# Ordering a two-layer decoder trunk by the tile context's timeline model instead of its core model

## The chip, the cores and the metric

The kernel runs on one core of a Trainium2 chip. The metric is the device time of one execution in microseconds (us). The core has TensorE (PE, with a separate row PEld for its weight loads), VectorE (DVE), ScalarE (ACT), GpSimd (POOL) and SyncE (SP, which issues the DMA transfers here). Each engine works through its own list of instructions in order. An instruction that waits for a semaphore holds up everything behind it on its engine.

## The reference, cut to what matters

Two layers over x of 1024 tokens by 1024 features, all in float32:

```python
h = x @ w_in                                   # 1024 x 2912
o_sb   = stick_breaking_attention(q, k, v)     # 4 heads of 64, causal
o_mla  = mla_mixer(...)                        # 4 heads, causal softmax attention
o_rwkv = rwkv7_mixer(...)                      # 8 heads of 64, a linear recurrence over time
mix = concatenate([o_sb, o_mla, o_rwkv]) @ w_o
x = layer_norm(ALPHA * x + mix)
u_act, u_gate = split(x @ ffn_w_up, 2)
hid = gelu(causal_depthwise_conv(u_act)) * u_gate
x = layer_norm(ALPHA * x + hid @ ffn_w_down)
```

Stick-breaking attention multiplies each score's weight by the product of "keep" factors of all later keys, which is a scan along the keys. The recurrence is `state = state*w - (state@kk)*(kk*a) + v*k`, with the output `state @ r` at each of the 1024 steps.

## The kernel before

The code is one long Python function that emits instructions in program order inside a tile context. The tile context knows which instruction needs which tile, adds the semaphores, and then **chooses the order of instructions on each engine** with a model of the machine: among the instructions that its model holds ready, it takes the one that stands earliest in the program, shifted by the numbers of a table `PRIORITY` (L38 to L50; `rw_chain_q` 80 and `rw_chain_s` 40 go forward, `rw_chain_y2` -60 goes back). So the order on the chip comes from that model. [...]

Float32 products are made of three matmuls on split operands (`mm3`, L202 to L204: high by high, high by low, low by high), each 128x512. A name with `psmm` is such a matmul of a dense projection or of the feed-forward network (FFN).

A layer goes through these parts, named here as the prediction names them:

- **Prefix.** `phase_a` makes the projections of the softmax attention and of the recurrence, and for each of four feature tiles (`ft`) the first stage `rw_stage1` (transposes, then L662 on PE, masks on DVE at L665 and L666, then L674 on PE). The last L674 ends the prefix. The recurrence is done in chunks of 64 tokens, and each chunk needs the inverse of a triangular matrix. `rw_inv` makes it for a pair of feature tiles: on DVE a transposition L701, a forward substitution in small steps L705 and L706, and a transposition L726; then a row of hand-overs: PE L735, ACT L738, POOL L740, DVE L743, PE L752, ACT L755, PE L764 (on `LA<-xxd`, loaded by DMA L760), ACT L765, and DMA L768 to the DRAM buffer `psd`. It is run twice a layer, once within the prefix and once behind it.
- **Serial stretch.** `rw_chain(0)` runs the recurrence for the first pair of feature tiles: per step two DMA loads `PSl<-psd` L807 and `RBl<-rbd` L808, PE L820, DVE L821 and L822 with ACT L823, then the state `S`: PE L839, DVE L842, which the next step needs. The second inverse is interleaved with it.
- **Second chain.** `rw_chain(1)` needs the `psd` of the second inverse. In the program it stands among `proj_sb` (L260), the six dense projections of the stick-breaking attention: 288 `psmm` matmuls, which need nothing but x and weights.
- **Attention.** The softmax streams (`mla`, scores L202 to L204 and L539 into `pssc`) and the stick-breaking streams (`stick`: scores PE L376 and L377 into `pspq` and `pspy`, ACT L378, POOL L384, DVE L385, L387 and L388 on the tile `mexp`, then PE L327, which transposes `mexp`, ACT L328, PE L312).
- **Output projection and FFN.** `oproj` and `ffn`: thousands of `psmm` and `psps` matmuls.

The buffers bound how far work can be pulled forward: `pst` holds four projection results, `PSl` and `RBl` two steps, `mexp` three blocks, `wt4` six blocks.

## Time and profile before

| | |
|---|---|
| median of 3 runs (3151.39 to 3157.18) | 3154.57 us |
| the profiled execution's own time | 3154.05 us |
| its span in the trace | 3152.3 us |
| PE busy | 2993.2 us, 95% |
| DVE busy | 1796.4 us, 57% |
| ACT busy | 1058.6 us, 34% |
| POOL busy | 330.7 us, 10% |
| mean granted TensorE clock, share of full speed | 0.981 |

"Busy" is the time in which an engine had an instruction under way; the rest of the span it sat idle. The granted clock is the share of 2.4 GHz at which TensorE was allowed to run: 1.00 is 2.4 GHz all the time, 0.50 would be 1.2 GHz all the time. A mean over a stretch mixes the two levels. The span plus 1.75 us is the execution's time.

### The profile page before, as it was taken

How to read it: one execution, taken by the hardware profiler on the slowest of the kernel's cores; microseconds unless marked ns; L12 is line 12 of the kernel's file. 1: busy time of each engine (PE TensorE's matmuls, PEld its weight loads, DVE VectorE, ACT ScalarE, POOL GpSimd, SP SyncE). 2: the span in 40 equal slices, each digit the busy share in tenths (PEclk: the TensorE clock that was granted, in tenths of full speed). 3: DMA queues.
4: the chain of work that ended last, by engine and by line, in shares of the span. 5: the costliest groups of instructions: out<-in, count | busy, mean ns of one | idle time of the engine just before them, and what ended most of it. 6: DMA issues, size and time to landing. Idle time of an engine off the chain costs nothing. (4 is left out here: it accounts for less than half of the span.)

```text
span 3152.3 us, 42021 instructions
## 1 busy us (share of the span) xinstructions
PE 2993.2 (95%) x16572; PEld 2421.2 (77%) x16572; DVE 1796.4 (57%) x2842; ACT 1058.6 (34%) x1865; POOL 330.7 (10%) x346
## 2 busy tenths in 40 slices
PE   8998999988999999999999989999789999999998
PEld 6677777776888888888877767777678888888887
DVE  4587764876644444444746877567865444344436
ACT  5444343764122112222144443446532211122220
POOL 0112131132000000000001111311310000000000
PEclk9999899999999999999999999999899999999999
DMA  4344566323421111111234456662235111111111
GB/s 129 97 141 110 169 186 191 97 62 121 149 85 50 51 41 47 54 50 51 64 84 127 108 132 193 178 190 53 81 121 172 54 47 40 43 56 49 54 47 54
DMA packets 339284, 301.79 MB, mean 96 GB/s; under 512 B 25224, under 2 KB 304016, under 8 KB 339088
## 3 DMA queue, kind: packets, MB, share of 16 engines
q1 hardware_dynamic: 339088, 299.11, 32.1%
q8 instruction: 131, 2.15, 0.3%
q14 instruction: 65, 0.53, 0.1%
HBM read 208.87 MB, written 90.18 MB: 95 GB/s over the span
## 5 line engine op out<-in xcount | busy, mean ns | idle before, releaser
L202 PE MATMUL psmm<-xTh,whi 128*128 128x512 f32 x2144 | 852.9, 398 | 0.0
L204 PE MATMUL psmm<-xTh,wlo 128*128 128x512 f32 x2144 | 852.1, 397 | 0.0
L203 PE MATMUL psmm<-xTl,whi 128*128 128x512 f32 x2144 | 852.1, 397 | 0.0
L197 ACT CAST whi<-raw 128x1024 fp32r<-128x1024 f32 x152 | 159.9, 1052 | 1111.3 <-PE psmm L203 1076.1
L204 PEld LDWEIGHTS psmm<-xTh,wlo 128*128 128x128 f32 x2144 | 405.2, 189 | 93.2 <-issue 4.3
L202 PEld LDWEIGHTS psmm<-xTh,whi 128*128 128x128 f32 x2144 | 405.4, 189 | 92.9 <-issue 4.4
L203 PEld LDWEIGHTS psmm<-xTl,whi 128*128 128x128 f32 x2144 | 405.3, 189 | 92.8 <-issue 3.9
L198 DVE TENSOR_TENSOR wlo<-raw,whi 128x1024 fp32r<-128x1024 f32 x122 | 148.8, 1220 | 424.5 <-ACT whi L197 424.5
L1031 DVE TENSOR_TENSOR y<-y,psps 128x512 f32<-128x512 f32 x288 | 196.2, 686 | 171.8 <-PE psps L204 171.4
L202 PE MATMUL psps<-wdh,hh 128*128 128x512 f32 x672 | 266.8, 397 | 0.0
L203 PE MATMUL psps<-wdl,hh 128*128 128x512 f32 x672 | 263.1, 391 | 0.0
L204 PE MATMUL psps<-wdh,hl 128*128 128x512 f32 x672 | 260.1, 391 | 0.0
L894 POOL TENSOR_TENSOR lrs<-lrs,mhalf 128x1 f32<-128x1 f32 x32 | 29.1, 910 | 1637.7 <-DVE lrs L893 1637.7
L202 PEld LDWEIGHTS psps<-wdh,hh 128*128 128x128 f32 x672 | 126.1, 188 | 36.4 <-ACT hh L197 5.5
L204 PEld LDWEIGHTS psps<-wdh,hl 128*128 128x128 f32 x672 | 126.2, 188 | 27.0
L203 PEld LDWEIGHTS psps<-wdl,hh 128*128 128x128 f32 x672 | 126.3, 188 | 25.8
L1006 DVE TENSOR_TENSOR cv<-cv,psmm 128x1024 f32<-128x1024 f32 x44 | 53.7, 1221 | 143.3 <-PE psmm L204 138.4
L198 DVE TENSOR_TENSOR wdl<-raw,wdh 128x1024 fp32r<-128x1024 f32 x42 | 51.4, 1225 | 88.5 <-ACT wdh L197 88.5
L198 POOL TENSOR_TENSOR wlo<-raw,whi 128x1024 fp32r<-128x1024 f32 x30 | 76.0, 2532 | 242.5 <-ACT whi L197 242.4
L312 PE MATMUL pspa<-Aa,mv 128*128 128x128 f32 x576 | 86.4, 298 | 4.4 <-ACT Aa L328 3.8
L312 PEld LDWEIGHTS pspa<-Aa,mv 128*128 128x128 f32 x576 | 77.1, 207 | 17.5 <-ACT Aa L328 15.8
L820 PE MATMUL pspa<-RBl,PSl 128*128 128x128 f32 x512 | 73.4, 292 | 17.2 <-ACT QC L823 11.8
(443 smaller groups left out, 4777.4 us busy)
## 6 DMA issues: line engine op xcount, KB each, us to landing
raw<-in_ffn_w_up_dram SPq DMA_DIRECT2D x88, 512.0 KB
raw<-in_w_in_dram SPq DMA_DIRECT2D x44, 512.0 KB
raw<-in_ffn_w_down_dram SPq DMA_DIRECT2D x44, 512.0 KB
rbd<-RB SPq DMA_DIRECT2D x64, 256.0 KB
PSl<-psd SPq DMA_DIRECT2D x32, 512.0 KB
RBl<-rbd SPq DMA_DIRECT2D x32, 512.0 KB
psd<-Vz SPq DMA_DIRECT2D x64, 128.0 KB
xxd<-X SPq DMA_DIRECT2D x64, 128.0 KB
```

Source lines behind the costliest of these rows:

```text
L197: self.nc.scalar.copy(hi, src)
L198: (eng or self.nc.vector).tensor_tensor(lo, src, hi.bitcast(F32), op=ALU.subtract)
L202: mm(out, lh, rh, start=start, stop=False)
L203: mm(out, lh, rl, start=False, stop=False)
L204: mm(out, ll, rh, start=False, stop=stop)
L312: self.nc.tensor.matmul(av, V[:, j, :], wt[:, j, :], start=j == 0, stop=j == nb - 1)
L820: nc.tensor.matmul(pQ[:, f, e, :], PSh[:, f, h, e, :], RBh[:, f, h, e, :], start=True, stop=True)
L894: nc.gpsimd.tensor_tensor(rs, rs, self.mhalf[:, 0:1], op=ALU.pow)
L1006: nc.vector.tensor_tensor(cv, cv, pg, op=ALU.mult)
L1031: nc.vector.tensor_tensor(y[:, i, hs], y[:, i, hs], ps, op=ALU.add)
```

## The change

One argument of the tile context. The program (tiles, buffers, instructions with their operands, dependencies, the priority table) stays; the order on each engine is now chosen with a timeline model of the machine where it was a core model before.

```diff
@@ -1222,7 +1222,7 @@
     a["x"] = a["x"][0]
     out = nc.dram_tensor("out_0_dram", (1, S, D), F32, kind="ExternalOutput").ap()
     a["out"] = out[0]
-    with tile.TileContext(nc) as tc:
+    with tile.TileContext(nc, schedule_with_timeline_sim=True) as tc:
         build(tc, a)
     r = _run(nc, [arrays], core_ids=[0])
```

Both programs hold 13 948 matmuls. Listed with equal neighbours in one row, PE's order has 11 484 rows before and 11 402 now, and 11 219 lines differ between the two lists; DVE's has 2678 and 2664, with 3409 lines of difference. Three places on PE show the pattern, all in layer 1. A name's number tells the tiles of one buffer apart.

The first is the start of the serial stretch, the first steps of `rw_chain(0)`. `psmm_4041` belongs to the projections, `pspa` and `pspy` to the chain. Before:

```order
L820 MATMUL pspa_3214<-RBl_3205,PSl_3206 128x128 x4
L820 MATMUL pspa_3222<-RBl_3205,PSl_3206 128x128 x4
L204 MATMUL psmm_4041<-xTh_130,wlo_4010 128x512
L202 MATMUL psmm_4041<-xTh_130,whi_4009 128x512
L203 MATMUL psmm_4041<-xTl_131,whi_4009 128x512
L204 MATMUL psmm_4041<-xTh_130,wlo_4010 128x512
...
L202 MATMUL psmm_4041<-xTh_130,whi_4009 128x512
L820 MATMUL pspa_3260<-RBl_3251,PSl_3252 128x128 x4
L820 MATMUL pspa_3268<-RBl_3251,PSl_3252 128x128 x4
L839 MATMUL pspy_3230<-S_528_3187,QC_3213 64x64 x4
```

and now, where `psmm_4690` is the last projection tile that still stands here:

```order
L204 MATMUL psmm_4690<-xTh_130,wlo_4659 128x512
L820 MATMUL pspa_3214<-RBl_3205,PSl_3206 128x128 x4
L820 MATMUL pspa_3222<-RBl_3205,PSl_3206 128x128 x4
L820 MATMUL pspa_3260<-RBl_3251,PSl_3252 128x128 x4
L839 MATMUL pspy_3230<-S_528_3187,QC_3213 64x64
L820 MATMUL pspa_3268<-RBl_3251,PSl_3252 128x128 x4
L839 MATMUL pspy_3230<-S_528_3187,QC_3213 64x64 x3
L820 MATMUL pspa_3330<-RBl_3321,PSl_3322 128x128 x4
L839 MATMUL pspy_3230<-S_529_3191,QC_3213 64x64 x4
```

Before, projection matmuls stand between the chain's steps, and this goes on through the whole serial stretch; now the steps follow one another. Counted in the order, 315 `psmm` matmuls stood between the last L674 of the prefix and the first L327 of the stick-breaking attention (56 up to the first L820, 74 from there to the second inverse's first L735, 106 to the second chain's first L820, 79 behind that). Now 51 are left there, all ahead of the first L820. The other 264 are in the prefix: 789 stood ahead of the last L674, now 1053. Layer 2 has the same counts.

The second is the end of the second inverse and the first L820 of the second chain (`pspa_4079`), as it is now:

```order
L875 MATMUL pspa_3997<-ident_60,yn_3995 128x128
L876 MATMUL pspa_3997<-sg_3128,g_520_3120 128x128
L764 MATMUL pspi_3910<-LA_3908,Aa_877 128x128 x4
L764 MATMUL pspi_3916<-LA_3908,Aa_877 128x128 x4
L764 MATMUL pspi_3968<-T_3966,Aa_877 128x128 x4
L764 MATMUL pspi_3974<-T_3966,Aa_877 128x128 x4
L820 MATMUL pspa_4079<-RBl_4070,PSl_4071 128x128 x4
L820 MATMUL pspa_4087<-RBl_4070,PSl_4071 128x128 x4
L820 MATMUL pspa_4125<-RBl_4116,PSl_4117 128x128 x4
L839 MATMUL pspy_4095<-S_528_3187,QC_4078 64x64
```

In this piece 106 `psmm` matmuls stood before between the inverse's L735 and `pspa_4079`; now there is none, and the inverse's and the second chain's instructions meet directly.

The third is a block of the stick-breaking attention. Its scores are `pspq_6188` and `pspy_6192`, its tile is `mexp_6187`, and its first transpositions are the last row. Before:

```order
L376 MATMUL pspq_6188<-kh_944_5413,qh_943_5412 128x512
L377 MATMUL pspq_6188<-kl_945_5414,qh_943_5412 128x512
L376 MATMUL pspy_6192<-kh_944_5413,qh_943_5412 128x384
L377 MATMUL pspy_6192<-kl_945_5414,qh_943_5412 128x384
L202 MATMUL pssc_6226<-kh_920_5311,qh_918_5309 128x128
L203 MATMUL pssc_6226<-kl_921_5312,qh_918_5309 128x128
L327 MATMUL pspa_6117<-ident_60,mexp_6102 128x128 x4
L327 MATMUL pspa_6123<-ident_60,mexp_6102 128x128 x4
...
L376 MATMUL pspq_6363<-kh_944_5413,qh_943_5412 128x512
L327 MATMUL pspa_6202<-ident_60,mexp_6187 128x128 x4
```

and now:

```order
L376 MATMUL pspq_6188<-kh_944_5413,qh_943_5412 128x512
L377 MATMUL pspq_6188<-kl_945_5414,qh_943_5412 128x512
L376 MATMUL pspy_6192<-kh_944_5413,qh_943_5412 128x384
L377 MATMUL pspy_6192<-kl_945_5414,qh_943_5412 128x384
L312 MATMUL psav_5770<-Aa_4944,mv_4951 128x128
L327 MATMUL psav_5816<-ident_60,mexp_5805 128x128 x4
L202 MATMUL pssc_6010<-kh_907_5277,qh_905_5275 128x384
L203 MATMUL pssc_6010<-kl_908_5278,qh_905_5275 128x384
L204 MATMUL pssc_6010<-kh_907_5277,ql_906_5276 128x384
...
L312 MATMUL pspa_6129<-Aa_4944,mv_5237 128x128 x4
L327 MATMUL pspa_6202<-ident_60,mexp_6187 128x128 x4
```

Before, 27 matmuls stand between the block's last score matmul and its first transposition. Now there are 106, of other blocks and of the other attention. Between the attention's first and last L327 stood 3 `psmm` matmuls before and stand 48 now: 45 of `oproj`, which stood behind the attention. On DVE, between the last L665 of the prefix and L726 of the second inverse, there were 24 state updates L842 and 12 of L821; now there are 16 and 10.

## Rows read from the trace of the kernel before

**Rows 1.** The page: its span, and the busy time of each engine.

```profile
span 3152.3 us, 42021 instructions
PE 2993.2 (95%) x16572; PEld 2421.2 (77%) x16572; DVE 1796.4 (57%) x2842; ACT 1058.6 (34%) x1865; POOL 330.7 (10%) x346
```

**Rows 2.** Stretches: length, each engine's busy us (instructions), granted clock, DMA share, GB/s.

```profile
core 0: us, PE busy (x) PEld busy (x) DVE busy (x) ACT busy (x) POOL busy (x), PEclk, DMA share, GB/s
144.00:365.00 221.00, 201.63 (x1467) 160.06 (x1467) 163.92 (x284) 100.80 (x199) 44.39 (x46) 0.94 0.47 131
250.00:270.00 20.00, 15.77 (x69) 12.80 (x68) 20.00 (x29) 5.38 (x12) 4.18 (x2) 0.87 0.21 53
365.00:431.00 66.00, 59.58 (x457) 47.30 (x454) 60.98 (x117) 21.64 (x39) 13.68 (x9) 0.95 0.65 206
378.00:390.00 12.00, 6.14 (x36) 5.37 (x35) 10.93 (x24) 3.98 (x5) 0.00 (x0) 0.76 0.51 168
431.00:487.00 56.00, 52.79 (x547) 43.90 (x540) 20.00 (x39) 23.14 (x44) 20.48 (x19) 0.97 0.60 167
487.00:584.00 97.00, 89.41 (x697) 71.85 (x698) 61.07 (x168) 48.75 (x114) 14.91 (x18) 1.00 0.60 182
545.00:550.00 5.00, 3.77 (x35) 2.94 (x34) 3.42 (x10) 2.21 (x3) 0.65 (x1) 1.00 0.90 229
584.00:745.00 161.00, 142.27 (x971) 122.71 (x969) 126.26 (x234) 101.86 (x277) 39.03 (x48) 0.95 0.21 57
745.00:1576.00 831.00, 825.46 (x3653) 674.32 (x3652) 399.49 (x482) 170.71 (x177) 18.13 (x16) 1.00 0.22 70
2045.00:2134.00 89.00, 80.47 (x666) 66.77 (x666) 57.35 (x158) 46.55 (x110) 15.73 (x18) 1.00 0.62 192
2134.00:2304.00 170.00, 144.41 (x1001) 125.66 (x1001) 131.33 (x245) 104.25 (x280) 39.38 (x48) 0.95 0.21 57
```

**Rows 3.** Timeline: the two instructions that end the prefix and begin the attention's transpositions.

```profile
start us, us, engine line op out<-in xcount [idle before <-releaser]
364.63 0.45 PE L674 MATMUL pspa<-Vz,Aa 64*64 64x64 f32 x8
...
583.68 0.27 PE L327 MATMUL pspa<-ident,mexp 128*128 128x128 f32 x1
```

**Rows 4.** Stretches, `psmm` instructions alone: PE, PEld, DVE, ACT, clock, DMA, GB/s.

```profile
365.00:431.00 66.00, 34.70 (x130) 23.37 (x130) 1.62 (x3) 3.68 (x6) 0.95 0.65 206
431.00:487.00 56.00, 27.93 (x106) 19.12 (x106) 0.00 (x0) 2.34 (x4) 0.97 0.60 167
487.00:549.00 62.00, 24.68 (x79) 13.99 (x79) 0.00 (x0) 2.35 (x4) 1.00 0.57 185
```

**Rows 5.** Timeline: three dense matmuls in a row, in the last FFN.

```profile
3060.07 0.40 PE L203 MATMUL psmm<-xTl,whi 128*128 128x512 f32 x1
...
3060.31 0.39 PE L204 MATMUL psmm<-xTh,wlo 128*128 128x512 f32 x1
...
3060.54 0.40 PE L202 MATMUL psmm<-xTh,whi 128*128 128x512 f32 x1
```

**Rows 6.** Groups on DVE, 365 to 431: busy us, mean ns, idle before.

```profile
L705 DVE TENSOR_TENSOR pd<-LA,T 128x2 f32<-128x2 f32 (+18 forms) x19 | 13.5, 710 | 0.6
...
L821 DVE TENSOR_TENSOR QC<-pspa,arl 64x256 f32<-64x256 f32 x12 | 5.1, 421 | 2.0 <-PE pspa L820 1.8
...
L842 DVE TENSOR_TENSOR S<-pspy,Gc 64x128 f32<-64x128 f32 x12 | 3.5, 289 | 0.3
```

**Rows 7.** Timeline: the second inverse's hand-overs, to the second chain's first L820.

```profile
430.63 1.20 PE L735 MATMUL pspi<-LA,Aa 32*32 32x32 f32 x64
...
435.66 3.52 POOL L740 MEMSET Aa<- 128x4096 f32 x1 [1.28 <-PE pspi L735]
...
470.47 1.13 PE L764 MATMUL pspi<-LA,Aa 128*128 128x128 f32 x8 [0.43 <-DMA LA<-xxd]
...
482.31 0.81 SPq L807 DMA_DIRECT2D PSl<-psd  x2
...
487.24 2.02 PE L820 MATMUL pspa<-RBl,PSl 128*128 128x128 f32 x16 [0.79 <-DMA PSl<-psd]
```

**Rows 8.** Waits of PE, 584 to 745: total us, times, longest us.

```profile
PE pspa L327 <- DVE mexp L388: 9.8, 9, 3.1
```

## The prediction

> **What bounds the kernel now.** First the page's line of busy times [rows 1]: PE works 2993.2 of 3152.3 us, so only 159 us are PE's idle time, and no other engine is above 57%. An order that changes no instruction can gain at most that idle time, plus what a low clock costs. The prediction therefore needs to know where these 159 us lie, and whether the new order gathers more of them.
>
> The table of stretches comes second [rows 2]. From 745 to 1576, the output projection and FFN of layer 1, PE is busy 825.46 of 831 us at clock 1.00: no order can win anything there. The idle time lies in the mixers: 19.4 us in 144 to 365 (the prefix behind its first projections), 9.8 us in 365 to 487 (the serial stretch), 7.6 in 487 to 584 (second chain), 18.7 in 584 to 745 (attention). Layer 2 shows 8.5 in its second chain and 25.6 in its attention. The cuts are the last L674 and the first L327 [rows 3] and the second chain's first L820 [rows 7].
>
> The third view asks what kind of work fills these stretches. Of the serial stretch's 122 us, DVE holds the first half: 60.98 of 66 us, most of it the small steps of the forward substitution [rows 2, 6]. The second half is a row of hand-overs, PE to ACT to POOL to DVE to PE, and two trips through DRAM, from 430.63 to 487.24 [rows 7]; there DVE is busy only 20.0 of 56 us, and no engine but PE is near full. PE's fullness is made by `psmm` matmuls, which the recurrence doesn't need: 34.70 + 27.93 us of their time in 365 to 487 [rows 4]. The chain sets the length of this stretch, and the dense matmuls are work that rides along for nothing.
>
> **The price of one dense matmul.** Three in a row start at 3060.07, 3060.31 and 3060.54, so one costs (3060.54 - 3060.07) / 2 = 0.235 us of PE [rows 5]; the busy time of a row (0.40) overlaps its neighbour. I use 0.233, the step over longer runs of the same kind.
>
> **The sum, part by part, for layer 1 and layer 2.**
>
> *A, the prefix.* 264 matmuls come in: 264 x 0.233 = 61.6 us. They replace waits there where they can. The most to be won is the idle time and the clock: 221.0 - 201.63 = 19.4 us, and 6% of 221 = 13 us, together 32 us [rows 2]. Against that, part of this idle time lies in places that DVE fills (250 to 270: DVE 20.00 of 20.00, PE 15.77), and I take 14 of the 32. A = +48 us, bounds +30 (all filled) and +62 (none).
>
> *B, the serial stretch, 122 us.* It loses its filler but not its chain. Eight L842 and two pairs of L821 and L822 fewer stand ahead of the inverse on DVE: 8 x 0.289 + 2 x 2 x 0.42 = 4.0 us [rows 6]. Dense matmuls no longer stand in front of the hand-overs: some ten hops at up to one matmul's 0.40 us make 4 us at most. Against these stands PE's clock. In 378 to 390 PE was busy 6.14 of 12 us and the granted clock was 0.76, a mixture of 1.2 and 2.4 GHz after waits [rows 2]; without filler more of the stretch looks like that. What remains on PE here is some 50 us (112.4 less 62.6), and at 0.76 it would take 16 us more, were all of it on the path. I take B = 0; bounds -8 and +16.
>
> The Trainium skill speaks against this change here: "TensorE: Matmul & The Clock Gate", section "HAM oscillation — how this bites in real kernels", says that a kernel whose bursts of matmuls are separated by waits starts each burst at the lower clock again. By it B would cost near +16 in each layer and the total would come out some 32 us higher. The trace has a row on each side: 378 to 390 agrees with 0.76, while 545 to 550, chain without filler and PE busy 3.77 of 5, was granted 1.00 [rows 2].
>
> *C, the second chain.* 79 matmuls leave it: 18.4 us [rows 4, 5]. PE needs 89.4 - 18.4 = 71.0 us then, and DVE's 61 us lie below that, so in layer 1 nearly all is won: -18. Layer 2's stretch is 89 us with DVE 57.35 and the same chain, so less is to be had: -12. Bounds -20 and -9 (half, if the chain's own steps set the pace).
>
> *D, the attention.* A stick-breaking block's scores go through ACT, POOL and three DVE passes before PE can transpose them. Between a block's last score matmul and its first transposition stood 27 other matmuls in the block shown, 106 now; at 142.27 / 971 = 0.147 us each [rows 2] that is 4.0 us of cover before and 15.6 now (over all these blocks the middle one goes from about 5 to 12 us). PE waited 9.8 us at nine of these places [rows 8]. DVE's 126 of 161 us [rows 2] is far enough from full to let this go. I take half of PE's idle time: -9 and -13, bounds -20 and +5 (if a block that starts earlier only waits for a buffer).
>
> *E, the output projection.* 45 of its matmuls fill the attention's last waits: 45 x 0.233 = 10.5 us that no longer follow: -10.5, bounds -12 and 0.
>
> Layer 1: 48 + 0 - 18 - 9 - 10.5 = +10.5. Layer 2: 48 + 0 - 12 - 13 - 10.5 = +12.5. Sum +23 on the profiled execution's 3154.05 us, which stands 0.5 us below the median: **3177 us**, slower by 0.7%. In words: 125 us of covering work leave a stretch that doesn't get shorter, and the places that they go to, or leave, give back about 100.
>
> **The rivals.**
>
> *The prefix takes the filler for nothing (faster).* If the moved matmuls fall into waits of stage 1, where each L662 waits for masks on DVE before L674, A is +30; with B -8, C -20, D -18, E -11 a layer gains 27 and the time is 3154 - 54 = 3100. It decides the sign once the prefix absorbs over 61.6 - (18 + 9 + 10.5) = 24 us a layer. For it: clock 0.94 and 19.4 us of idle time there. Against it: DVE is busy 163.9 of 221 us and full in the place shown, and dense work on PE doesn't make DVE faster.
>
> *The bare stretch falls to the lower clock (much slower).* B +16, C 5 dearer (its 97 us at 0.95, as the attention has it, in place of 1.00), A 8 dearer, as fewer waits fill: 10.5 + 29 = +39 a layer, 3154 + 78 = 3232. For it: the row at 0.76. Against it: the row at 545 to 550.
>
> *Gains and losses cancel (no change).* A +37 in place of +48 and the rest as taken: 3154, within 6 us either way.
>
> *That the order doesn't change* is excluded: 11 219 lines of PE's order differ.
>
> **How the numbers follow.** 0.2% of 3154 is 6.3 us, about what a measurement of this kernel can tell from no change. My forecast, slower by 0.2 to 1.7%, has 0.40; the bare stretch at the lower clock 0.12; no change 0.12; the prefix that absorbs it, faster, 0.36. So slower 0.52, same 0.12, faster 0.36. All bounds at their low ends give -8 + 30 - 20 - 20 - 12 = -30 a layer, 3094; at their high ends 62 + 16 - 9 + 5 + 0 = +74, 3302, but the two layers and five parts won't all fall one way. The range 3095 to 3245 takes in the faster rival at 3100 and the slow one at 3232. The likeliest case alone spans 3160 to 3210.
>
> **What would show it.** In the changed profile, cut at the same instructions: the last L674 some 48 us later, at about 413; from there to the second chain's first L820 still about 122 us, with no `psmm` behind its first 12 us, PE busy falling towards half and the granted clock below 0.95; from that L820 to the first L327 about 79 us; the attention about 152 us, with the waits of L327 on L388 under half of the 9.8 us; the FFNs unchanged at 831. The prediction is wrong if the prefix ends before 395 (then A was mis-sized and the kernel is likely faster), if the serial stretch shrinks well below 110 us (then filler had been holding up the chain and B is a gain), or if the attention grows, since blocks started early may only hold buffers that others need.

## The result: slower by 2.7%, and the profile after

The changed kernel takes 3237.35 us (median of 4 runs, 3230.15 to 3243.27), the kernel before 3152.98 us in the same set; the ratio is 1.0266 (95% interval 1.0240 to 1.0291). The forecast had the sign and the range right, but its 3177 us are 60 us short: it put the loss at 23 us, and it is 84.

The page's first lines of the changed kernel, span and busy time of each engine, answer to [rows 1]:

```profile
span 3237.9 us, 42087 instructions
PE 3020.0 (93%) x16572; PEld 2491.6 (77%) x16572; DVE 1776.4 (55%) x2842; ACT 1056.0 (33%) x1865; POOL 314.9 (10%) x346
```

The span grew by 3237.9 - 3152.3 = 85.6 us. PE's idle time went from 159.1 to 217.9 us, 58.8 more. The other 26.8 us are PE's busy time: the same 16 572 records took longer, and the mean granted clock fell from 0.981 to 0.952. So about two thirds of the loss is waiting, and one third is PE being busy for longer. The lower clock has a part in that third (by the clock records of the two traces PE was busy at 1.2 GHz for 222 us, before for 95); how large a part isn't shown, for matmuls that stand apart count for more busy time too (0.40 us each, and a step of 0.235 in a row [rows 5]).

The stretches of the changed kernel, cut at the same instructions as in [rows 2] (last L674, the second chain's first L820, first L327 of the stick-breaking attention, last L327), layer 1 and then layer 2, with two short pieces at the end:

```profile
core 0: us, PE busy (x) PEld busy (x) DVE busy (x) ACT busy (x) POOL busy (x), PEclk, DMA share, GB/s
144.00:427.60 283.60, 263.22 (x1670) 209.01 (x1668) 162.36 (x278) 110.34 (x209) 49.68 (x50) 0.91 0.41 117
427.60:545.80 118.20, 82.61 (x806) 71.60 (x804) 74.12 (x149) 32.02 (x67) 21.62 (x22) 0.74 0.55 169
545.80:636.10 90.30, 72.80 (x618) 64.39 (x619) 65.44 (x180) 49.88 (x120) 16.48 (x19) 0.88 0.68 193
636.10:786.90 150.80, 139.50 (x1013) 128.27 (x1011) 127.93 (x226) 104.64 (x274) 39.04 (x49) 0.97 0.25 69
1752.10:2034.30 282.20, 257.15 (x1647) 205.43 (x1646) 162.07 (x275) 108.62 (x206) 49.36 (x49) 0.91 0.42 115
2034.30:2149.90 115.60, 80.02 (x806) 69.39 (x804) 72.47 (x149) 32.22 (x67) 21.79 (x22) 0.75 0.58 173
2149.90:2242.90 93.00, 73.70 (x607) 65.04 (x608) 66.19 (x179) 49.49 (x117) 16.13 (x19) 0.87 0.66 187
2242.90:2396.00 153.10, 139.19 (x1025) 128.12 (x1023) 129.98 (x227) 106.13 (x278) 38.40 (x49) 0.98 0.25 68
280.00:307.30 27.30, 20.53 (x99) 17.02 (x98) 25.06 (x47) 9.63 (x22) 1.86 (x3) 0.50 0.33 97
526.00:550.00 24.00, 11.80 (x51) 10.59 (x51) 1.16 (x4) 2.92 (x5) 1.90 (x2) 0.51 0.47 132
```

Read the first row against [rows 2, 144 to 365]: 283.6 us in place of 221.0, and the idle time in it is 20.4 us in place of 19.4. The prefix took the matmuls in, but hardly any of its waits were filled. The second row is the bare serial stretch: 118.2 us, four less than before, with PE busy 82.6 of it where it was 112.4, at clock 0.74. The third is the second chain: 18.4 us of matmuls left it, and yet it takes 90.3 us against 96.4. The fourth is the attention, 150.8 us, the one place that got clearly shorter. Layer 2 says the same, but for its second chain, which got longer (93.0 us against 89.3).

What cover did can be read at one instruction, the second chain's first L820, whose wait is the last of the serial stretch. Waits of PE over the whole run, and the timeline of the changed kernel there, from the second inverse's last L764:

```profile
PE pspa L820 <- DMA PSl<-psd: 19.1, 2, 9.6
```

```profile
534.10 2.08 PE L764 MATMUL pspi<-T,Aa 128*128 128x128 f32 x8 [0.72 <-ACT T L765]
545.80 4.86 PE L820 MATMUL pspa<-RBl,PSl 128*128 128x128 f32 x24 [9.62 <-DMA PSl<-psd]
```

Before, PE waited 0.79 us at this place [rows 7], and that L764 was

```profile
476.04 1.11 PE L764 MATMUL pspi<-T,Aa 128*128 128x128 f32 x8
```

From its end to L820 it was 10.1 us then and is 9.6 now: the way was no shorter before, but dense matmuls ran while the transfer was under way. The waits of L327 on L388 [rows 8], on the other hand, are gone from the attention.

### The profile page after: what moved, and what is told of

Its sections match the earlier page's. It is cut to its first block, busy times and chain, and to the rows that moved or that the text cites. A ratio compares the mean times of both kernels' runs of the same rounds, so it can differ in the third digit from the quotient of the medians.

```text
span 3237.9 us, 42087 instructions
## 1 busy us (share of the span) xinstructions
PE 3020.0 (93%) x16572; PEld 2491.6 (77%) x16572; DVE 1776.4 (55%) x2842; ACT 1056.0 (33%) x1865; POOL 314.9 (10%) x346
## 5 line engine op out<-in xcount | busy, mean ns | idle before, releaser
L820 PE MATMUL pspa<-RBl,PSl 128*128 128x128 f32 x512 | 90.5, 336 | 43.4 <-DMA PSl<-psd 19.1
L820 PEld LDWEIGHTS pspa<-RBl,PSl 128*128 128x128 f32 x512 | 79.5, 238 | 49.4 <-ACT QC L823 19.9
L312 PE MATMUL psav<-Aa,mv 128*128 128x128 f32 x576 | 83.4, 284 | 8.6 <-ACT Aa L328 8.5
L1001 ACT ACTIVATE cv<-cv 128x1024 f32<-128x1024 f32 x44 | 46.7, 1061 | 135.1 <-DVE cv L1000 135.0
```

The lines of the kernel that those rows point to most:

```text
L312: self.nc.tensor.matmul(av, V[:, j, :], wt[:, j, :], start=j == 0, stop=j == nb - 1)
L820: nc.tensor.matmul(pQ[:, f, e, :], PSh[:, f, h, e, :], RBh[:, f, h, e, :], start=True, stop=True)
L1001: nc.scalar.activation(cv, cv, AF.Gelu)
```

## The experiments

Two edits recur. `issue_after` and `add_manual_dep` with `NoSync` add an edge to the order alone: the second instruction stands behind the first on its engine, and nothing waits for a result. Whole orders can be set that way. What no edge holds, the model orders anew, so that stages which an edit doesn't name can change too. All ratios are to runs of the kernel before on the same chip.

### 1 and 2. Hold the matmuls back; push them ahead in the order of before

The first kernel is the changed one with this:

```diff
+        with self.tc.issue_after(self.l674.ins):
             sg = self.sg = self.proj_rw(l, 13, kp, "sg")
...
+        with self.tc.issue_after(self.l674.ins):
             self.proj_sb(l, pp, cstep)
```

> The timeline order, with the projections of the stick-breaking attention and the one of sg held on PE behind the prefix's last L674 (issue order alone, no wait); all the rest is left to the timeline model. Theory 1, displaced cover: the 264 matmuls are free behind the recurrence and cost 0.233 us each in the prefix. Then the prefix gets back its 62 and 72 us, the serial stretch stays within 5 us of 118 and 116 with the filler back in it, the attention keeps its 152 and 154, and the time is 3105 to 3135, faster than before. Theory 2, spacing: what costs in the prefix is how the timeline model spaces stage 1, not the matmuls that came in; then the prefix gets back at most a third and the time is above 3190. Theory 3, clock: the loss is PE's lower clock in the bare stretches; then the granted clock returns to 0.975 or more, the prefix gets back only about 20 us a layer, the serial stretch and the second chain shrink by 15 us a layer, and the time is 3155 to 3180.

3208.23 us, ratio 1.0173 (1.0158 to 1.0189). Only 29 us came back: neither theory 1's 3105 to 3135 nor theory 3's 3155 to 3180, and theory 2's time. But the prefix got back 35.6 us in layer 1 (279.0 to 243.4 between its first and last L674) and 45.1 in layer 2, more than theory 2 gave it, and the serial stretch grew to 145.7, since all 336 matmuls were now in it:

```profile
148.50:391.90 243.40, 208.49 (x1362) 166.85 (x1361) 151.95 (x269) 95.86 (x188) 36.14 (x44) 0.79 0.41 115
391.90:537.60 145.70, 132.14 (x1088) 109.17 (x1089) 88.72 (x155) 45.11 (x85) 33.48 (x27) 0.96 0.54 168
```

Without the displaced matmuls the prefix is still 243 us against 213.7 before, with 35 us of idle time and a clock of 0.79. So there are two costs, and the second was not among my theories in that form.

The second kernel is the one before, with edges the other way round (the projections ahead of L674):

```diff
+        self.behind(self.kv[3, 0, 1], self.lmm)
...
+                self.behind(self.kv[3, 1, 0] if i < 2 else self.kv[3, 1, 1], self.lmm)
```

> The order of before, with the reverse done by issue-order edges on PE: sg and four projections of the stick-breaking attention have to be issued ahead of the last L674 groups of the prefix, so that 219 matmuls a layer (not 264) come ahead of its end; the attention keeps the order of before. Theory 1: the prefix ends 51 us a layer later (219 x 0.233), the serial stretch stays near 122, the second chain gives back about 6, and the time is 3153 + 2 x 45 = 3243, range 3220 to 3260. Theory 2: little changes, under 3180. Theory 3: as theory 1 in sign, but the lengthening sits in the serial stretch and the second chain (clock under 0.85 there, each some 15 us longer), and the prefix grows by less than 35.

3212.09 us, ratio 1.0186 (1.0168 to 1.0204). Its prefix and serial stretch, and the second chain:

```profile
151.40:414.60 263.20, 245.24 (x1654) 193.72 (x1654) 180.96 (x307) 108.16 (x207) 48.79 (x49) 0.96 0.44 126
414.60:525.70 111.10, 80.68 (x849) 66.82 (x849) 62.60 (x120) 33.14 (x70) 23.66 (x23) 0.86 0.60 185
525.70:602.70 77.00, 66.34 (x569) 56.32 (x570) 55.33 (x154) 43.00 (x99) 14.76 (x17) 0.91 0.65 198
```

The prefix grew by 263.2 - 213.7 = 49.5 us, and 219 matmuls at 0.233 are 51.0: theory 1 within 2 us, at clock 0.96, which takes theory 3 out of this prefix. The chain behind gave back more than expected (19 us in the second chain, 11 in the serial stretch), so that the whole is +57 and not +90, 8 us below theory 1's range. Displacing 219 of the 264 matmuls, with the rest of the order left to the core model, is worth 57 us, its attention 6.1 and 4.6 us longer than before included.

### 3 and 4. Leave the matmuls out, in either order

```diff
-        for k in range(KT):
-            self.mm3(pt, hi[:, k, :], ..., k == 0, k == KT - 1)
+        for k in range(kt):
+            self.mm3(pt, hi[:, k, :], ..., k == 0, k == kt - 1)
```

with `kt` 1 for the stick-breaking projections: seven of their eight feature blocks are left out.

> The order of before, with seven of the eight feature blocks of the six stick-breaking projections left out (the matmuls on feature block 0 stay, 36 of 288 in each layer, so the values are not the reference's): 252 matmuls or 58.7 us of PE work fewer a layer. Theory 1: they were free in this order except behind the second chain (79 x 0.233 = 18 us at most), so the time falls by 0 to 2 x 18: 3117 to 3153. Theory 2: the same as theory 1. Theory 3: the stretches are bare now as in the changed kernel, PE falls to the lower clock there, and the time stays at 3150 to 3180 although 117 us of work are gone.

> The timeline order with the same matmuls left out. Theory 1: here they stand in the prefix and cost their full time, so the time falls by 2 x 55 to 2 x 62 from 3237 to 3113 to 3127, below or level with the order of before without them, and the difference between the two orders is gone. Theory 2: it falls by at most 2 x 20, and stays above 3190. Theory 3: the bare stretches stay as cold as they are, the prefix gains the matmuls' time less what it waits: 3130 to 3150, and the clock in the serial stretch stays under 0.85.

The order of before: 3169.22 us, ratio 1.0049 (1.0034 to 1.0064). 117 us of PE work were taken out, and the kernel became 15 us **slower**. The timeline order: 3187.33 us, ratio 1.0109 (1.0092 to 1.0126), 50 us less than with the matmuls. The same work was worth less than nothing in the one order and 50 us in the other. That fits displaced cover, but doesn't show it alone: the first time lies in theory 3's range (3150 to 3180) and not in theory 1's, and the second missed theory 1's figure (3113 to 3127) by 60 us, so the two orders don't become equal without the matmuls. The rest was ordered anew besides: in the first kernel the attention of layer 1, which lost no matmul, takes 173.6 us in place of 161.1. The lean kernel's serial stretch in the order of before:

```profile
363.50:496.50 133.00, 83.89 (x816) 71.12 (x816) 84.33 (x155) 45.14 (x85) 34.94 (x27) 0.76 0.61 186
```

It is 11 us longer than with the filler, at clock 0.76 (before 0.95 and 0.97, [rows 2]), as theory 3 had said.

### 5 and 6. Hold the recurrence's own projections too

The trace of the changed kernel showed a second shift: 618 dense matmuls stand ahead of the second half of the second feature tile's stage 1, in place of 499, and the first inverse's L701 begins at 254 us in place of 215. Kernel 5 holds k, r and v of a feature tile behind the L674 of the first half of the one before; kernel 6 does both holds.

> The timeline order, in which k, r and v of each feature tile of the recurrence are held on PE behind the L674 of the first half of the feature tile before (issue order alone); sg and the stick-breaking projections are left free. It undoes the other shift, found in the first four runs: some 120 of the recurrence's own projection matmuls came ahead of the second feature tile's stage 1, so that the first inverse began at 254 in place of 214. Of 264 matmuls that had come ahead of the last L674, 168 remain. Theory 1, displaced cover: the inverse begins at 215 to 222, the prefix takes 245 to 255 in place of 279 (214 and 168 x 0.233 = 39 less what waits take up), and the time is 3170 to 3195. Theory 3, clock: where PE's matmuls stand does not matter, only how cold PE is; the prefix shrinks by less than 12 us and the time stays above 3210.

> Both holds together, with the two V projections of the stick-breaking attention held behind the second chain's first L820 besides, so that PE's dense matmuls stand about where they stood before (768 ahead of the last L674, 240 in the serial stretch, 96 in the second chain); everything else is the timeline order. Theory 1: prefix 214 to 224, serial stretch 118 to 128, second chain 90 to 97, attention 152 and 154 as in the changed kernel (before 161 and 170), tail 842: 3120 to 3150, below before. Rival, the rest of the timeline order (spacing of stage 1, order on VectorE) is slower by itself: above 3165.

3209.80 us (1.0169, 1.0149 to 1.0188) and 3215.78 us (1.0196, 1.0173 to 1.0218). Both miss theory 1. In kernel 5 the inverse begins at 245 us and the prefix is 272.8 us, only 6 less than in the changed kernel; that little, and the time, are about what theory 3 gave. In kernel 6, with the dense matmuls counted out about as before, the prefix is 251.8 and 242.5 us, against 213.7 and 209.8, and the inverse still begins at 251. Theory 1 does not cover this second cost; the rival of kernel 6 ("the rest of the timeline order is slower by itself") is what was measured.

### 7 and 8. Keep PE warm with dummy matmuls

```diff
+    def warm(self, pt):
+        for _ in range(4):
+            self.nc.tensor.matmul(pt, self.xTh[:, 0, 0:P], self.xTh[:, 0, 0:512], start=True, stop=True)
+        return pt
...
-            pQ = self.pst("pa").rearrange(...)
+            pQ = self.warm(self.pst("pa")).rearrange(...)
```

> The timeline order with four dummy matmuls (128x512, read by nobody, overwritten by the real product) ahead of each group of the chains' L820 and of the second inverse's L735, L752 and L764: 176 a layer, 41 us of PE work more, in stretches where PE sat idle 35 and 38 us. It holds PE's clock up without moving anything else. Theory 3: the granted clock rises above 0.93 there, the serial stretch falls from 118 to 108 or less, the second chain from 90 to 80 or less, and the time is 3205 or less. Theory 1: the clock rises, but these stretches stay within 4 us of what they were or grow, since DVE and the hand-overs set their length: 3225 to 3270.

> The order of before without the 252 stick-breaking matmuls a layer (as in the lean run at 3169, so the values are not the reference's), with the same 176 dummy matmuls a layer in the chains and the second inverse. In the lean run the serial stretch took 133 us at clock 0.76, 11 longer than before, though PE had less to do. Theory 3: with the dummies the clock is above 0.93, the serial stretch 120 to 126 and the time 3125 to 3150, faster than the lean run although PE does 82 us more. Theory 1: the 11 us are not the clock's; the serial stretch stays at 133 or more and the time is 3169 or above.

3276.88 us (1.0386) and 3219.06 us (1.0199): both on theory 1's side, kernel 7 even 7 us above its range. In kernel 7 the serial stretch's clock rose from 0.74 to 0.91, and it took 127.4 us in place of 118.2:

```profile
430.40:557.80 127.40, 98.05 (x922) 82.29 (x920) 76.19 (x149) 32.00 (x67) 20.46 (x22) 0.91 0.49 149
```

This doesn't clear the clock altogether. The dummies stand in front of products on the path: 12 groups of the second inverse at 4 x 0.233 = 0.9 us are 11 us, more than the 9 by which the stretch grew. And the two attentions, where no dummy stands, grew by 15 us. It shows that a warm PE bought with work on the path isn't worth it, not that the cold costs nothing.

### 9 and 10. Dense matmuls between the steps of stage 1

In the changed kernel, L662, L665 and L674 of stage 1 stand like this on PE (timeline, engine PE; VectorE's L665 for this group ran from 241.49 to 241.90):

```profile
240.24 1.16 PE L662 MATMUL pspa<-q,q 64*128 64x128 f32 x8
...
243.01 0.50 PE L202 MATMUL psmm<-xTh,whi 128*128 128x512 f32 x1
...
246.37 0.40 PE L204 MATMUL psmm<-xTh,wlo 128*128 128x512 f32 x1
246.70 0.45 PE L674 MATMUL pspy<-Vz,Aa 64*64 64x64 f32 x8
```

The masked product that L674 needs was there at 241.90, and 15 dense matmuls later, at 246.70, PE came to it.

> Theory 4, formed after the first eight runs: the timeline order puts runs of 14 to 18 dense matmuls (3.5 to 5 us) between the steps of stage 1 (PE L662, DVE L665, PE L674), where the hand-over itself takes about 1 us; so stage 1 of a feature tile takes 43 us in place of 20, the first inverse begins at 251 to 254 in place of 214, and the dense matmuls that should cover it are spent by then. This kernel is the run with both holds, but k, r and v of a feature tile are held behind the last L674 of the whole feature tile before, so that no dense matmul can stand between the steps of stage 1. Theory 4: stage 1 takes 20 to 25 us, the first inverse begins before 230, the prefix ends by 380 (397 with both holds) and the time is below 3190 (3216 with both holds), though PE sits idle in every hand-over. Rival: the order on VectorE and ScalarE stretches stage 1; then it stays near 40 us, the first inverse begins after 245, and the time is 3210 or more.

> The order of before, in which the four groups of L674 of the second feature tile's stage 1 are held on PE behind the 24th, 48th, 72nd and 96th of the third feature tile's projection matmuls (issue order alone). It puts about 50 more dense matmuls between the steps of stage 1, ahead of the first inverse, and nothing else. Theory 4: the first inverse begins 10 to 16 us later than 214, the prefix ends 8 to 16 us later, and the time is 3165 to 3185. Rival: the matmuls have to be done anyway and the inverse finds other cover; the prefix ends within 4 us of before, the time within 6 us of it.

Kernel 9: 3253.09 us, 1.0320 (1.0305 to 1.0336). Kernel 10: 3136.36 us, 0.9947 (0.9933 to 0.9961). Both go against theory 4, which falls; kernel 10's rival (within 6 us of before) missed too, for the kernel is 18 us faster. Stage 1 did become shorter in kernel 9: the second feature tile's L674 run from 216.0 to 239.3, 23 us, in place of 212.5 to 255.2, 43 us, with both holds. But its first inverse began at 238.3 for that, and the prefix took 262.4 us, with one spell of 47.8 us at half the clock:

```profile
144.20:406.60 262.40, 231.75 (x1464) 184.75 (x1463) 164.27 (x274) 99.79 (x193) 41.14 (x46) 0.81 0.39 110
279.70:327.50 47.80, 34.22 (x334) 28.77 (x335) 38.62 (x51) 14.85 (x36) 8.43 (x5) 0.50 0.37 109
```

And kernel 10, in which the first inverse began 14 us later (229.2), ended its prefix 7 us earlier: with the third tile's projections done, PE's idle time in it fell from 17.6 to 11.4 us. The start of the first inverse isn't what sets the prefix's end.

### 11. One number of the priority table

```diff
-    "w_transpose": -10,
+    "w_transpose": -100,
```

> The order of before with one number of the priority table changed, w_transpose from -10 to -100, which puts more matmuls of other blocks between an attention block's scores and its transposition, as the timeline order does. If the attention's gain of 10 and 17 us in the changed kernel comes from this lag, the attention takes 150 to 156 here (161 and 170 before) and the time is 3125 to 3140, faster than before. Rival: that gain belongs to the timeline order as a whole or to the 45 matmuls of the output projection; then the time is within 6 us of before.

3150.19 us, 0.9988 (0.9979 to 0.9997): the rival. A lag set by that number brings at most 0.2%; its attention took 173.8 us in layer 1 and 172.8 in layer 2, longer than before, though the waits of L327 on L388 (20.3 us in the whole run before) are gone from it altogether. The attention of layer 1:

```profile
580.50:754.30 173.80, 152.60 (x1039) 132.17 (x1038) 135.19 (x241) 107.90 (x288) 35.98 (x50) 0.95 0.25 67
```

PE is idle for 21.2 us of it, before for 18.7 [rows 2]; 30 more matmuls of the output projection stand in it (some 7 us). So without these waits the attention is not yet shorter.

### 12, 13 and 17. PE's order and the other engines' orders, swapped

The order of an engine is read from one program and set in the other, as edges between neighbours:

```diff
+    for text in ORDERS:
+        names = [f"I-{n}" for n in np.frombuffer(zlib.decompress(base64.b85decode(text)), dtype=np.int32)]
+        for x, y in zip(names, names[1:]):
+            tc.add_manual_dep(ins[y], x, info, reason="order")
```

> The core model again, but PE's instructions are held, one behind the other, in exactly the order of the changed program (issue order alone); VectorE, ScalarE, GpSimd and SyncE are ordered by the core model around it. Theory 5: the whole loss sits in PE's order (where the dense matmuls stand); 3220 to 3255, with the stages of the changed kernel (prefix 279, serial 118, second chain 90, attention 151). Rival: it sits in the order of the other engines (stage 1 on VectorE and ScalarE, the transfers on SyncE); then below 3190.

> The reverse: the timeline model, with PE's instructions held in exactly the order of before. Theory 5: 3145 to 3170, with the stages of before (prefix 214, serial 122, second chain 96, attention 161). Rival, the other engines' order: above 3190.

> The timeline model, with PE's instructions from the projections to the second chain (both layers, nothing of attention or FFN) held in exactly the order of before. The run with PE's whole order of before (3247) brought the prefix back to 222 and 225 but lost in the later stages, where PE's order of before and the other engines' timeline order didn't fit. Theory 5: the loss of the changed kernel sits in PE's order up to the second chain; prefix 220 to 226, serial stretch 122 to 134, second chain 96 to 112, attention 150 to 155, tail 842: 3150 to 3190. Rival: the other engines' order costs as much there; above 3215.

3330.34 us (1.0550), 3246.59 us (1.0295) and 3185.82 us (1.0092, 1.0073 to 1.0112). The first two miss theory 5 on the total, and kernel 13's is where its rival put it: PE's order from one model beside the other engines' orders from the other is worse than either model throughout in kernel 12, and no better than the changed kernel in kernel 13 (the intervals overlap). Kernel 13 lost 10 to 14 us against before in each serial stretch and second chain; kernel 12 lost another 12 and 6 us against the changed kernel in the prefixes and 16 and 10 in the second chains. On the prefix they agree with it. PE's timeline order makes it 291.0 and 288.6 us among engines ordered by the core model; PE's order of before makes it 221.6 and 225.0 among engines ordered by the timeline model:

```profile
149.50:371.10 221.60, 198.23 (x1435) 156.18 (x1435) 158.06 (x272) 96.33 (x191) 40.64 (x45) 0.92 0.46 130
```

Kernel 17, in which only PE's order up to the second chain is that of before, came out about as theory 5 had it: prefix 225.5 and 228.6, serial stretch 134.9 and 133.7, attention 153.8 and 155.5, and 51 of the 84 us are back.

### 16. The small matmuls' order alone

> The run with both holds (3216), with the small matmuls and transpositions of PE up to the inverses (those of the softmax projections' preparation, stage 1 and the inverses, but not the dense psmm) held among themselves in the order of before. In the run with both holds the prefix stayed at 252 and 243 though the dense matmuls were back. If the order of the small ones among themselves made that, the prefix is 213 to 225 here and the time below 3175. Rival: it is still where the dense ones stand among the small ones; then the prefix stays above 238 and the time above 3195.

3253.96 us, 1.0315 (1.0294 to 1.0336), prefix 267.0 and 260.7: the rival. The order of the small matmuls among themselves isn't the second cost, and with it the kernel is 38 us slower than kernel 6. With kernels 6, 9 and 13 that leaves, by elimination, the places of the dense matmuls among them.

### 14 and 15. The attention's order alone, and with the fill of kernel 10

> The core model, with the instructions of the attention alone (both kinds, on all five engines) held among themselves in the order of the changed program; prefix, chains and FFN are as before. If the attention's gain belongs to that order and not to what stands around it, the attention takes 150 to 156 us in both layers (161 and 170 before), the rest is as before, and the time is 3120 to 3138, the fastest of all. Rival: it gained only because less was left to do beside it; then 3145 or more.

> The attention's order of the changed program (as in the run at 3119) together with the four issue-order edges on the second feature tile's stage 1 (as in the run at 3136). The two act on different stretches: if they add, the prefix takes 203 to 206 and 198 to 202 (214 and 210 before), the attention 144 to 148, and the time is 3098 to 3110. Rival: the prefix's gain comes back as a longer second chain; then 3115 to 3125.

3119.48 us, ratio 0.9880 (0.9865 to 0.9894), and 3102.54 us, 0.9837 (0.9824 to 0.9851): kernel 14 half a us below the range expected, kernel 15 within it, and both faster than either kernel. By stage it came otherwise: the attention won more than expected, and the second chain wasn't as before. The attention of kernel 14 in layers 1 and 2:

```profile
592.60:737.80 145.20, 134.17 (x995) 124.36 (x994) 126.29 (x230) 104.53 (x275) 40.41 (x49) 0.98 0.25 70
2131.90:2277.70 145.80, 132.76 (x1004) 122.27 (x1003) 129.75 (x235) 105.52 (x278) 42.09 (x50) 1.00 0.26 72
```

PE's idle time is 11 and 13 us, against 18.7 and 25.6 [rows 2]; 16 and 24 us are won there, some 12 of them in each layer lost again in the second chain, and 18 won in the FFNs and projections behind. Kernel 15 has the shortest prefix of all, 200.5 us:

```profile
152.00:352.50 200.50, 189.51 (x1435) 149.11 (x1435) 152.74 (x272) 96.41 (x191) 40.50 (x45) 0.98 0.50 144
```

## Why the prediction was wrong in size

The terms of the sum against the two traces, cut at the same instructions (us, layer 1 / layer 2; A counts from the start in layer 1 and from the first L674 in layer 2, E is all that lies behind the attention up to the next layer's first L674 or the end):

| term | forecast | measured |
|---|---|---|
| A, prefix | +48 / +48 | +62.5 / +72.4 |
| B, serial stretch | 0 / 0 | -4.0 / -6.5 |
| C, second chain | -18 / -12 | -6.1 / +3.7 |
| D, attention | -9 / -13 | -10.3 / -16.7 |
| E, output projection | -10.5 / -10.5 | -3.1 / -6.4 |
| sum | +23 | +85.5 |

In this cut 50 of layer 2's 264 matmuls, those ahead of its first L674, count in layer 1's E, and 214 in layer 2's A.

**What held.** Covering work left a stretch that doesn't get shorter without it. In the bare serial stretches PE's idle time grew by 26 and 25 us (35.6 us in each, against 9.9 and 10.8), and they gave back 4.0 and 6.5 us; B was even a little cheaper than taken. Kernel 2 shows the same in the order of before: its prefix grew by nearly the full price of the matmuls pushed into it.

**The step that failed first is A's "I take 14 of the 32".** It credits the prefix with a part of its idle time and of its clock, and neither was won. Of the 264 matmuls, 50 did go ahead of the first L674, and in layer 1 that part grew no longer, it shrank by 2.8 us. Behind it came 214 matmuls, 50 us at 0.233. From first to last L674, before (both layers) and changed (layer 1; layer 2 stands above):

```profile
151.40:365.10 213.70, 196.15 (x1435) 155.79 (x1435) 156.85 (x272) 96.65 (x191) 41.68 (x45) 0.94 0.49 136
1713.00:1922.90 209.90, 190.49 (x1435) 152.01 (x1436) 157.76 (x272) 96.56 (x192) 39.24 (x45) 0.95 0.52 139
```

```profile
148.60:427.60 279.00, 258.62 (x1647) 205.31 (x1646) 161.00 (x275) 108.68 (x206) 48.52 (x49) 0.91 0.41 117
```

The 65.3 us of layer 1 are 62.5 us of PE's busy time and 2.8 of idle time, the 72.3 of layer 2 are 66.7 and 5.6. So the matmuls cost their full price, PE was busy for another 13 and 17 us, and on balance no wait was filled. The lower clock has a part in the 13 and 17, of a size not shown: half-speed spells of 51 us in each prefix, against 27 and 20 before. A third of the idle time of layer 1's prefix lies in 280 to 307.3, where DVE is busy 25.06 of 27.30 us and no dense matmul stands on PE before 303.1. I had named such a place (250 to 270) and still credited a part of it. A's upper bound, +62, was too low, for it took the clock as something to be won and not to be lost, and layer 2 lies 10 us above it.

**The second is C.** "Nearly all is won" rested on PE's busy time, 89.4 - 18.4 = 71.0 us, and that came out: 72.8. But these matmuls, too, had been cover. PE's idle time grew from 7.4 to 17.5 us (layer 2: 8.5 to 19.3). Waits of PE in layer 1's second chain, first before, then now:

```profile
PE pssc L202 <- ACT mexp L546: 0.7, 2, 0.4
PE pspa L820 <- ACT QC L823: 0.6, 1, 0.6
```

```profile
PE pssc L202 <- ACT mexp L546: 3.9, 3, 2.7
PE pspy L839 <- ACT QC L823: 3.6, 1, 3.6
PE psav L312 <- ACT Aa L328: 2.4, 1, 2.4
PE pspa L820 <- ACT QC L823: 1.4, 2, 1.3
PE pspa L875 <- ACT QC L823: 1.3, 1, 1.3
PE pspq L839 <- ACT QC L823: 0.6, 1, 0.6
```

The chain's waits for `QC` are 6.9 us, the softmax streams' for ACT 6.3. In kernel 2 the second chains did get 19.4 and 13.3 us shorter. But its attentions got 6.1 and 4.6 us longer (in layer 1 some 49 other instructions of PE went there from the second chain); second chain and attention together won 13.3 and 8.7 us, less than the 16.4 and 13.0 of the changed kernel.

**D has the right size, but not for a reason that is shown.** The waits of L327 on L388 are gone, as forecast; in kernel 11 they are gone too, and its attention got longer. Kernel 14 shows only that the gain belongs to the attention's order as a whole, and there some 12 us of it in each layer come back in the second chain.

**E** can be read in layer 2 alone: 45 matmuls fewer gave 6.4 us there in place of 10.5. In layer 1 they left, and 50 of layer 2's projections came in.

One reading of the prediction was too strong as well: L705 and L706, the small steps, are 29.9 of DVE's 60.98 us in 365 to 431, which is half and not "most of it".

**The rivals.** The slow one, "the bare stretch falls to the lower clock", gave 3232 and had 0.12; the time is 3237. That it came so near is luck: its sum for layer 1 has A +56, B +16 and C -13, and measured are +62.5, -4.0 and -6.1. Its fact is right: the serial stretches have a clock of 0.74 and 0.75. The Trainium skill, "TensorE: Matmul & The Clock Gate", section "HAM oscillation — how this bites in real kernels", has bursts of matmuls that are separated by waits start at the lower clock each time. The row at 526 to 550, a wait of 9.62 us within it, agrees with 0.51. The cold was on the path too: the second inverse's four groups of L764 took 8.0 us in all, 4.4 before. But the stretch as a whole did not get longer by it. Kernel 2's bare serial stretch was 7 us shorter than this one, at clock 0.86; whether by the clock or by its order isn't shown. The faster rival needed a prefix that absorbs over 24 us a layer; on balance it absorbed none.

**What stays open.** Kernel 2 puts displacement, with 219 of the 264, at 57 us. The 27 us that the changed kernel lost beyond that are a balance. Against kernel 2, over both layers, its prefixes from first to last L674 are 36 us longer and its serial stretches 11, while second chain and attention together are 7 us shorter and all the rest 13. The longer prefix goes with PE's order (kernels 13 and 17), not with the small matmuls' order among themselves (kernel 16). Which places of the dense matmuls among them make it was not settled: fewer between the steps of stage 1 was slower (kernel 9), and more was faster in the order of before (kernel 10). What the lower clock costs was not settled either: kernel 7 raised it only by work on the path. The other engines' timeline order costs 8 to 19 us in each prefix and 10 to 13 in each serial stretch by kernels 13 and 17, but only beside PE's order of before, so that a share of its own can't be read off.

## What to carry to other kernels

Ask of dense work not what it costs but what it covers: before moving it, find which stretch it leaves, and whether that stretch gets shorter without it. An order that does dense work early uses up the cover that a later stretch, bound by another engine, would need. And a scheduler's switch is no single change: the attention's part of this order was worth 1.2% alone while the whole cost 2.7%, so take it apart by stage before it is kept or dropped.

## What the runs showed of the hardware

A stretch with less work on PE can run at a lower clock and take longer: with 504 matmuls fewer (16 068 records in place of 16 572) and the rest ordered anew, the serial stretch of the kernel before went from clock 0.96 to 0.76 and from 122.2 to 133.0 us, though PE was busy for 84 us of it in place of 112. The same eight 128x128 matmuls L764 took 1.11 us at 2.4 GHz before and 2.08 us in a spell at 1.2 GHz now. And PE can stay at 1.2 GHz while it works most of the time: in kernel 9 for 47.8 us in one piece, busy 34.2 of them, and in the changed kernel for 27.3 us, busy 20.5, whereas the longest such spell before was 10.2 us.
